# adaLN slots of the feed-forwards: eight running sums with an outside sum by TensorE, or row-wise multiply-and-sum on VectorE

## The chip, the core and the metric

The kernel runs on one core of a Trainium2 chip. The metric is the device time of one execution in microseconds (us). Engines are named as in the profile: PE is TensorE (PEld its weight loads), DVE is VectorE, ACT is ScalarE, POOL is GpSimd, SP is SyncE, which here issues nearly all the loads.

## The reference

Two transformer blocks of two layers each run over 256 tokens of 1024 features. Each layer has an adaLN vector of 6 x 1024 outputs, made from one condition vector; the change is only about how these vectors come about.

```python
def adaln(c, w_mod, b_mod):
    mod = jax.nn.silu(c) @ w_mod + b_mod          # [1, 6*1024]
    return jnp.split(mod, 6, axis=-1)             # shift, scale, gain; twice

def modulate(x, g, shift, scale):
    return rmsnorm(x, g) * (1.0 + scale[:, None, :]) + shift[:, None, :]

def swiglu(h, wg, wu, wd):
    return (jax.nn.silu(h @ wg) * (h @ wu)) @ wd
...
    # layer_ab, layer_c (block one): mixer, then
    h = modulate(x, norm_ffn, sh_f, sc_f)
    return x + g_f[:, None, :] * swiglu(h, wg, wu, wd)
```

Block one is `layer_ab` (a linear recurrence and sparse attention) and `layer_c` (attention over selected keys), each followed by `swiglu` with 2816 hidden features. Block two has two layers with a context of 256 more tokens, low-rank attention and 16 experts; its adaLN is computed for two condition vectors (tokens and context).

## The kernel before

Activations lie feature-major: 128 features on the partitions, 8 chunks, 256 tokens along the free axis. A dense product in fp32 is made from two rounded halves: `split` copies 1024 columns of a weight to a high half on ACT (`wsh`, L308) and subtracts it on DVE for the low half (`wsl`, L309), with three buffers of each; `mm3` (L316 to L318) then multiplies high by high, high by low and low by high.

A feed-forward (`ffn`) takes its norm first: the sum of squares on PE, a transpose to a narrow layout on DVE (L559), a reciprocal square root in tiny DVE operations of 8 columns (L567, L536 to L546), the way back (L577, L579), and then `h` (L604 on DVE, L605 on ACT, L606 on DVE). The gate/up part has 11 steps; each loads one 2 MB slot and makes two pairs of chunks, gate and up, of 24 products each, with the activation behind them (L973 on ACT, L974 and L975 on DVE, L976 on ACT, L977 on DVE). The down part has 8 chunks of 66 products. FFN0 runs from about 170 us of the trace, FFN1 from about 505 us; layer 1 of block one is between them, block two starts at about 710 us.

Loads go through `slot`: a ring of four places of 2 MB in block one, filled in the order of the program by SP's queue. A load waits until the place's former content has been read, and every load behind it on SP's queue waits with it. Where work on the former content has been put off, `slot` has that work emitted before it takes the place.

The adaLN vectors of the four layers (`mod0`, `mod1`, `ada0`, `ada1`) are 12 slots of 512 outputs each, made by the generator `mods` one after another, wherever the code calls `fill`. A slot on TensorE is 8 products of 128x32 by 128x512 (L458, 16 records in the trace), added up on DVE or ACT (L464, L462), and a transpose of all such slots at the end (L471). A slot on DVE is put off into a queue, `vq`, of eight pieces for each condition vector: one multiply-and-add of 128x512 each (L425; the first piece is ACT's, L428), and at the end four products with a column of ones on TensorE (L434) and an addition (L435). `split` takes three pieces from the queue after each split in gate/up (`VU`), one in down (`VD`). Strings set where slots go: `PF` after each gate/up step, `FD` before each down chunk, `NF` at the norms, `L1F` in layer 1's attention; a digit is that many slots on TensorE, `a` one on DVE.

Of the kernel before, what the change touches and what calls it, by code (L numbers as in the profile page):

```python
# [19 lines left out]
MC = 2  # L20
# [22 lines left out]
VU = 3  # L43
VD = 1
FD = 'a0aa0000,00000000'.split(",")
# [6 lines left out]
PF = [e for e in '02a0a00a0a0,2000000000a'.split(",")]  # L52
# [3 lines left out]
L1F = '0010020100000000'  # L56
NF = '021'
# [91 lines left out]
def layout(i):  # L149
# [30 lines left out]

    w = i["l0_w_in"]
# [53 lines left out]
class Kern:  # L235
# [41 lines left out]
    def slot(self, src, cuts=1):  # L277
        n = src.shape[-1]
        self.nslot += 1
        # a place is taken anew only when the work put off has had what is in it  # L280
        while any(e[2] is not None and self.nslot - e[2] >= len(self.rq_) for e in self.vq):
            self.pump(1)
        pool, tag, bufs = self.rq_.pop(0)
# [14 lines left out]
    def drop_ring(self, h):  # L298
        cm, mine = h
        self.pump(len(self.vq))  # L300
        self.rq_ = [e for e in self.rq_ if e not in mine]
        self.drop(cm)

    def split(self, src, n, tag=None):
# [5 lines left out]
        self.pump(self.vn)  # L310
# [25 lines left out]
    def setup(self):  # L336
# [20 lines left out]
        self.pend, self.vq, self.vn, self.nslot = None, [], 0, 0  # L357
        self.known = {}
# [47 lines left out]
    def mods(self, name, zname, bias):  # L406
        """The adaLN columns of one layer, a slot of 512 at a time; yields take the engine for the next."""
# [6 lines left out]
        for s in range(12):  # L414
            vec = yield
            w = self.slot(self.I[name][s].rearrange("p k n -> p (k n)"), MC if name == "mod0" and s == 3 else 1).rearrange("p (k n) -> p k n", n=512)
            z = self.zc[zname]
            old = self.mark("mods")
            if vec:
                zp, ts = self.zp, []  # L420

                def part(k, i, w=w, z=z, ts=ts, zp=zp):
                    c = 31 + 16 * i
                    if k:
                        nc.vector.scalar_tensor_tensor(ts[i], w[:, k, :], z[:, k, c:c + 1], ts[i], op0=ALU.mult, op1=ALU.add)  # L425
                    else:
                        ts.append(self.t(zp, [128, 512], F32, f"modv{i}", 1))
                        nc.scalar.activation(ts[i], w[:, 0, :], AF.Copy, scale=z[:, 0, c:c + 1])  # L428

                def fin(ts=ts, s=s):  # L430
                    for i, t in enumerate(ts):
                        tp = self.ps("t")
                        for q in range(4):
                            nc.tensor.matmul(tp[:, q:q + 1], t[:, q * 128:(q + 1) * 128], self.ones[:, 0:1], start=True, stop=True)  # L434
                        nc.vector.tensor_tensor(m[:, i, 4 * s:4 * s + 4], tp[:, :4], self.cols[:, o + 4 * s:o + 4 * s + 4], op=ALU.add)  # L435
                    self.known[name].add(s)

                for k in range(8):
                    for i in range(n):
                        self.vq.append((lambda k=k, i=i, part=part: part(k, i), "mods", self.nslot))  # L440
                f, old_ = self.vq[-1][0], fin
                self.vq[-1] = (lambda f=f, fin=fin: (f(), fin()), "mods", self.nslot)
                self.mark(old)
# [4 lines left out]
            if self.zp is None:  # L448
                # late: a window of its own
# [39 lines left out]
    def pump(self, n):  # L489
        """Some of the work put off for the vector engine."""  # L490
        for _ in range(min(n, len(self.vq))):
# [3 lines left out]
            self.mark(old)  # L495

# [8 lines left out]
    def flush(self, name=None, part=None):  # L505
        """The last steps of the adaLN columns, put off until they are asked for."""
        if name is None:
            self.pump(len(self.vq))
# [5 lines left out]
        while not need <= self.known[name]:  # L514
            assert self.vq, (name, part)
            self.pump(1)

# [16 lines left out]
    def rsqrt(self, y, c, t):  # L534
# [3 lines left out]
        # y (1 - e) ** -0.5 with e = 1 - c y y below 0.07, a polynomial to the last bits; scaled to a leading one  # L538
# [9 lines left out]
    def sums(self, x, gain=None):  # L548
        """Sum of the squares over the features; tokens 32 b + p on partition p, column b."""
# [23 lines left out]
    def spread(self, y):  # L573
        """A column layout of tokens back to a row on every partition."""
# [46 lines left out]
    def dense_iter(self, src, n, h, use, lead=0, cuts=1):  # L621
        """use(j, psum) for every 128-column chunk j of a packed weight [128, n, 1024]; the first ones by turns."""
# [18 lines left out]
    def lead(self, w, h):  # L641
        """Some chunks by turns, as the parts of h come."""
# [8 lines left out]
    def warm(self, n):  # L651
        """Products that keep the tensor engine's clock up while it waits."""
# [9 lines left out]
    def gelu(self, dst, src, n, eng=None):  # L662
        """dst = 2 * gelu(src)"""
# [35 lines left out]
    def lru1(self, axp, lruw):  # L699
# [5 lines left out]
        for c in range(4):  # L705
# [7 lines left out]
            # tr -> t = tanh(log_a / 2), rec -> 1 / (1 - t) = (1 + a) / 2  # L713
# [15 lines left out]
            # a = 1 + 2 t / (1 - t)  # L729
# [3 lines left out]
            # y = h * gelu(gate), gate holds 2 * gelu  # L733
# [10 lines left out]
    def attend(self, qch, qb, kz, mask, vtok, voff, gate, yps, first, last):  # L744
        """One pair of heads (one of either group), one block of queries."""
# [30 lines left out]
    def layer0(self, fill, r0, xr):  # L776
# [74 lines left out]
        # compressed keys and values  # L851
# [24 lines left out]
        # attention over the compressed keys  # L876
# [23 lines left out]
        for r in range(4):  # L900
# [28 lines left out]
            if r == LQ:  # L929
                self.mark("l0 lru")  # L930
                # xc -> sqrt(-t)
# [14 lines left out]
    def ffn(self, l, mname, fill):  # L946
        nc, I = self.nc, self.I
        self.mark("ffn")
        r = self.rstd(self.xT, 1024)
# [8 lines left out]
        self.vn = VU  # L958
# [24 lines left out]
        self.vn = VD  # L983
# [12 lines left out]
        self.vn = 0  # L996
        self.drop(fpc)

    def layer1(self, fill):
# [44 lines left out]
        def select(qb):  # L1044
# [14 lines left out]
            # causal keys only: v * m + (m - 1) * 3e38  # L1059
# [46 lines left out]
    def run_a(self):  # L1106
# [12 lines left out]
        def fill(n, vec=False):  # L1119
            if isinstance(n, str):  # L1120
                n, vec = (int(n), False) if n.isdigit() else (ord(n) - 96, True)
# [11 lines left out]
        if EN:  # L1133
            # the context's place is free
# [17 lines left out]
    def rs_cols(self, ss, n, inv):  # L1152
        """columns (ss * inv + eps) ** -0.5"""
# [10 lines left out]
    def rope(self, dst, src, t):  # L1164
        """src [128 tok, m, 64] -> dst"""
# [19 lines left out]
    def raw(self, nm, i=0):  # L1185
        """The slot of a packed weight, loaded at its first use."""
# [12 lines left out]
    def tm(self, acc, w, n, off, tiles, ks):  # L1199
        """Token-major products: acc[t][:, c0:] += h[t]^T w for some chunks of features."""  # L1200
# [19 lines left out]
    def st_v(self, sis):  # L1220
        """v and f"""
# [20 lines left out]
    def st_t(self, sis):  # L1242
        """Low-rank parts of queries, keys and values."""
# [53 lines left out]
    def st_k(self, si):  # L1297
        """Keys and values."""
# [39 lines left out]
    def st_q(self, si):  # L1338
        """Queries."""
# [36 lines left out]
        # (192 (ms + eps)) ** -0.5: norm and score scale  # L1376
# [12 lines left out]
    def st_s(self, si):  # L1389
        """Spatial gating."""  # L1390
# [15 lines left out]
    def st_f(self, si):  # L1406
        """Fourier transforms; the second half of the frequencies mirrors the first."""
# [20 lines left out]
    def st_a(self, si, hd):  # L1428
        """Attention of one head."""
# [30 lines left out]
    def st_w(self, sis, half=None):  # L1460
        """Output product, onto the residual."""
# [17 lines left out]
    def logits(self, i, s0):  # L1479
        """Four feature blocks' share of the logits of the scaled tokens, and of the sum of squares (row 16 of a quarter)."""  # L1480
# [16 lines left out]
    def st_x(self, si):  # L1497
        """Normed and modulated tokens (0) or context (1)."""
# [30 lines left out]
    def run_plan(self, plan):  # L1529
        """The stages of a layer of block 2 in the order in which they are traced."""  # L1530
# [73 lines left out]
    def st_p(self, si):  # L1604
        """What the route needs besides the tokens: scaled router weights, the shift's share of the logits."""
# [20 lines left out]
    def route(self, sis):  # L1626
        """Experts' choice and the tokens of the first experts, for some sets at once; in stages."""
# [301 lines left out]
```

## Time and profile before

| | |
|---|---|
| median of 3 runs | 1565.83 us (1565.28 to 1566.07) |
| profiled execution, span | 1562.8 us |
| outside the span, against the median | 3.0 us |
| PE busy | 1452.5 us (93%) |
| DVE busy | 845.4 us (54%) |
| ACT busy | 580.9 us (37%) |
| L458, the adaLN slots on TensorE | 624 records, 91.7 us busy |

"Busy" is the time in which an engine has at least one instruction in flight. The chain of work that ended last is followed backwards from the last instruction, so that its shares say on which engine the end of the program hung. Matmul records overlap; a record of 0.28 us follows the one before it after 0.12 us where PE runs without a break.

### The profile page before, as it was taken

How to read it: one execution, taken by the hardware profiler on the slowest of the kernel's cores; microseconds unless marked ns; L12 is line 12 of the kernel's file. 1: busy time of each engine (PE TensorE's matmuls, PEld its weight loads, DVE VectorE, ACT ScalarE, POOL GpSimd, SP SyncE). 2: the span in 40 equal slices, each digit the busy share in tenths (PEclk: the TensorE clock that was granted, in tenths of full speed). 3: DMA queues.
4: the chain of work that ended last, by engine and by line, in shares of the span. 5: the costliest groups of instructions: out<-in, count | busy, mean ns of one | idle time of the engine just before them, and what ended most of it. 6: DMA issues, size and time to landing. Idle time of an engine off the chain costs nothing.

```text
span 1562.8 us, 25643 instructions
## 1 busy us (share of the span) xinstructions
PE 1452.5 (93%) x10566; PEld 1001.6 (64%) x10566; DVE 845.4 (54%) x1960; ACT 580.9 (37%) x1184; POOL 5.6 (0%) x15
## 2 busy tenths in 40 slices
PE   5999999999999999999999998999998989897665
PEld 2975899998957899996754784434433655642211
DVE  5668787766776668745766542323224765421011
ACT  3455444443455444543654441111102564310000
POOL 0000000000000000000000000000000000000000
PEclk9999999999999999999999998999999999999888
DMA  9647767577464844545386976899994544799998
GB/s 398 259 181 288 269 225 294 195 291 289 144 262 164 312 174 155 189 170 189 115 317 226 402 308 250 332 414 386 412 368 168 201 175 182 313 429 427 427 427 346
DMA packets 33380, 432.55 MB, mean 277 GB/s; under 512 B 3696, under 2 KB 4336, under 8 KB 5872
## 3 DMA queue, kind: packets, MB, share of 16 engines
q1 hardware_dynamic: 32400, 429.92, 69.3%
q8 instruction: 83, 1.36, 0.3%
q10 hardware_dynamic: 864, 1.00, 0.2%
q14 instruction: 33, 0.27, 0.0%
HBM read 429.86 MB, written 1.05 MB: 276 GB/s over the span
## 4 chain that ended last, share of the span: by engine, by line
PE 79%; DMA 9%; DVE 6%; ACT 2%; issue 1%; POOLq 0%; DVEq 0%; ACTq 0%; SPq 0%
PE g L316 14%; PE g L317 14%; PE g L318 14%; PE g L1770 7%; PE y L1807 5%; DMA raw<-in_md_dram 4%; PE t L458 4%; DMA h<-in_mgu_dram 3%; DMA raw<-in_mgu_dram 3%; PE m L1770 2%; PE t L1729 2%; PE y L1441 1%; PE y L1439 1%; PE g L1457 1%; PE y L751 1%; PE y L1729 1%
## 5 line engine op out<-in xcount | busy, mean ns | idle before, releaser
L308 ACT ACTIVATE wsh<-raw 128x1024 fp32r<-128x1024 f32 (+4 forms) x236 | 243.2, 1033 | 323.9 <-PE g L317 228.3
L309 DVE TENSOR_TENSOR wsl<-raw,wsh 128x1024 fp32r<-128x1024 f32 (+4 forms) x236 | 280.2, 1189 | 147.5 <-ACT wsh L308 146.8
L316 PE MATMUL g<-h,wsh 128*128 128x256 f32 x1072 | 304.6, 286 | 2.8 <-ACT h L597 2.4
L318 PE MATMUL g<-h,wsl 128*128 128x256 f32 x1072 | 304.7, 285 | 0.6 <-DVE wsl L309 0.6
L317 PE MATMUL g<-h,wsh 128*128 128x256 f32 x1072 | 304.3, 285 | 0.1
L316 PEld LDWEIGHTS g<-h,wsh 128*128 128x128 f32 x1072 | 205.3, 192 | 8.0 <-ACT h L597 2.6
L318 PEld LDWEIGHTS g<-h,wsl 128*128 128x128 f32 x1072 | 206.0, 192 | 1.9 <-DVE wsl L309 1.0
L317 PEld LDWEIGHTS g<-h,wsh 128*128 128x128 f32 x1072 | 206.0, 193 | 1.9 <-DVE h L606 1.2
L1770 PE MATMUL g<-raw,xs 128*32 128x512 f32 x1232 | 166.9, 632 | 20.8 <-DMA raw<-in_mgu_dram 20.2
L1807 PE MATMUL y<-raw,a 128*32 128x512 f32 x736 | 100.4, 634 | 9.8 <-DMA raw<-in_md_dram 8.3
L1770 PEld LDWEIGHTS g<-raw,xs 128*32 128x32 f32 x1232 | 39.1, 113 | 106.2 <-issue 71.0
L316 PE MATMUL g<-gh,wsh 128*128 128x256 f32 x352 | 100.3, 285 | 0.0
L318 PE MATMUL g<-gh,wsl 128*128 128x256 f32 x352 | 99.7, 283 | 0.0
L317 PE MATMUL g<-gl,wsh 128*128 128x256 f32 x352 | 99.7, 283 | 0.0
L458 PE MATMUL t<-raw,zc 128*32 128x512 f32 x624 | 91.7, 621 | 5.5 <-DMA raw<-in_mod_dram 5.4
L1734 ACT ACTIVATE xs<-t,modada,ra 128x128 f32<-128x128 f32 x32 | 14.6, 457 | 152.5 <-PE t L1729 109.1
L316 PEld LDWEIGHTS g<-gh,wsh 128*128 128x128 f32 x352 | 67.5, 192 | 0.8 <-DVE modada L483 0.4
L317 PEld LDWEIGHTS g<-gl,wsh 128*128 128x128 f32 x352 | 67.5, 192 | 0.4 <-issue 0.4
L318 PEld LDWEIGHTS g<-gh,wsl 128*128 128x128 f32 x352 | 67.5, 192 | 0.4 <-issue 0.4
L1807 PEld LDWEIGHTS y<-raw,a 128*32 128x32 f32 x736 | 23.4, 112 | 63.7 <-issue 42.5
L1779 ACT ACTIVATE a<-g 128x512 f32<-128x512 f32 x12 | 7.2, 597 | 148.2 <-PE g L1770 148.2
L1732 DVE TENSOR_SCALAR xs<-t,ra,modada 128x128 f32<-128x128 f32 x32 | 13.1, 410 | 88.7 <-PE t L1729 50.4
(482 smaller groups left out, 2364.2 us busy)
## 6 DMA issues: line engine op xcount, KB each, us to landing
raw<-in_mgu_dram SPq DMA_DIRECT2D x61, 2048.0 KB, 13.1
raw<-in_md_dram SPq DMA_DIRECT2D x28, 2048.0 KB, 10.8
raw<-in_mod_dram SPq DMA_DIRECT2D x23, 2048.0 KB, 8.7
raw<-in_ada_dram SPq DMA_DIRECT2D x23, 2048.0 KB, 8.5
raw<-in_ffgu_dram SPq DMA_DIRECT2D x22, 2048.0 KB, 8.6
raw<-in_ffd_dram SPq DMA_DIRECT2D x16, 1408.0 KB, 5.9
raw<-in_win_dram SPq DMA_DIRECT2D x6, 2048.0 KB, 11.1
raw<-in_wo_dram SPq DMA_DIRECT2D x6, 2048.0 KB, 10.4
```

What stands on the lines that cost most here:

```text
L308: self.nc.scalar.activation(hi, src, AF.Copy)
L309: self.nc.vector.tensor_tensor(lo, src, hi.bitcast(F32), op=ALU.subtract)
L316: mm(out, ah, bh, start=first, stop=False)
L317: mm(out, ah, bl, start=False, stop=False)
L318: mm(out, al, bh, start=False, stop=last)
L458: nc.tensor.matmul(acc[32 * j:32 * j + 32, :], zw[:, k, :], w[:, k, :], start=(k < 4), stop=(k >= 4))
L751: nc.tensor.matmul(sc, qch[:, qb * 128:(qb + 1) * 128], kz[:, :, :nk], start=False, stop=True)
L1439: nc.tensor.matmul(sc, self.qT[:, hd, ts], self.kT[:, hd, :nk], start=True, stop=False)
L1441: nc.tensor.matmul(sc, self.qrT[s2, hd // 2, ts], self.krT[s2, hd // 2, :nk], start=False, stop=True)
L1729: nc.tensor.matmul(ps, s["ht"][:, t, k * 128:(k + 1) * 128], oh[:, t, :], start=(t == 0), stop=(t == 1))
L1770: nc.tensor.matmul(banks[si][u][32 * e:32 * e + 32, :], xs[:, k, e * 32:e * 32 + 32], raw[:, u * 2048 + e * 512:u * 2048 + e * 512 + 512], ...
L1807: nc.tensor.matmul(ys[si][32 * e:32 * e + 32, :], hts[si][:, f * 128 + 32 * e:f * 128 + 32 * e + 32], raw[:, (fj * 4 + e) * 512:(fj * 4 + ...
```

## The change

Slots given to DVE are now made row by row. The weights of all four layers are packed a second time, transposed (`mod0t` and so on), so that outputs lie on the partitions and the 1024 inputs along the free axis. One `tensor_tensor_reduce` (L438 of the new kernel, "ISA" in the rows below, followed by a row of 128x1 that writes the accumulated value) multiplies 128x1024 weights by the condition vector, which stands on every partition, and adds up each row: four of these make a slot for one condition vector, eight for two. Products with ones on TensorE are no longer needed. The product itself is written over the weights, or to a scratch tile in bfloat16 (`a512`) where the weights are needed again. The condition vector on all partitions (`crow`) is loaded at first use in a feed-forward by a DMA on ACT's queue and passed through ACT (Tanh) and DVE (L541).

The strings are new: eight DVE slots in FFN0's gate/up (four on DVE and two on TensorE before), three in its down part, six in FFN1's gate/up, where two on TensorE and one on DVE had been. `L1F` has one slot instead of four. In all 17 slots are on DVE instead of eight, and nine fewer on TensorE (two of these in layer 1 of block two). A split now takes 0.8 pieces from the queue. Code for slots on GpSimd is there and not used.

```diff
-VU = 3
-VD = 1
-FD = 'a0aa0000,00000000'.split(",")
+VU, VD = (0.8, 0.8), (0.8, 0.8)
+PU, PD = (0, 0), (0, 0)
+FD = ['d d d 0 0 0 0 0'.split(), '0 0 0 0 0 0 0 0'.split()]
...
-PF = [e for e in '02a0a00a0a0,2000000000a'.split(",")]
+PF = ['0 0 d d d d d d d d 0'.split(), 'd d d d d d 0 0 0 0 0'.split()]
...
-L1F = '0010020100000000'
-NF = '021'
+L1F = '0000000100000000'
+NF = '0,2,1'.split(',')
...
+        o[nm + "t"] = np.ascontiguousarray(w.T.reshape(12, 4, 128, 1024).transpose(0, 2, 1, 3))
...
-        self.pump(self.vn)
+        self.paced()
...
-                def part(k, i, w=w, z=z, ts=ts, zp=zp):
...
-                        nc.vector.scalar_tensor_tensor(ts[i], w[:, k, :], z[:, k, c:c + 1], ts[i], op0=ALU.mult, op1=ALU.add)
...
+                zr, ni = self.row(zname), 1 if name == "ada1" and s >= 4 else n
+                todo = [(q, i) for q in range(4) for i in range(ni)]
...
+                        junk = w[:, q, :] if last else self.w([128, 1024], "a512", NA5, BF16)
+                        nc.vector.tensor_tensor_reduce(junk, w[:, q, :], zr[:, i, :], 0.5, self.cols[:, o + 4 * s + q:o + 4 * s + q + 1],
+                                                       ALU.mult, ALU.add, m[:, i, 4 * s + q:4 * s + q + 1])
...
+    def paced(self):
+        self.vc += self.vn
...
+        self.pump(int(self.vc))
...
+    def row(self, zname):
...
+            nc.scalar.dma_start(z, self.I["crow"][:, :n] if n == 1 else self.I["crow"][:, 1:])
+            for i in range(n):
+                t = self.t(self.zr, [128, 1024], F32, "modp", 1)
+                nc.scalar.activation(t, z[:, i, :], AF.Tanh, scale=0.5)
+                nc.vector.scalar_tensor_tensor(z[:, i, :], t, 1.0, z[:, i, :], op0=ALU.add, op1=ALU.mult)
```

The final order on an engine is set by a scheduler, and it shows at three places. The first is DVE at FFN1's norm, from the transpose to the first row of `h`. Before:

```order
L559 STREAM_TRANSPOSE a_901_5590<-t_5565 128x256
L567 TENSOR_SCALAR rsc_5594<-t_5592 128x8
L536 TENSOR_SCALAR rsy_5596<-rsc_5594 128x8
L537 TENSOR_SCALAR rsy_5596<-rsy_5596 128x8
L539 TENSOR_TENSOR rst_5597<-rsy_5596 128x8
L540 TENSOR_TENSOR rst_5597<-rst_5597,rsc_5594 128x8
```

Now, in the same stretch (`raw_917` is the first slot of `ada0` on DVE, `crow` the condition vectors):

```order
L613 STREAM_TRANSPOSE a_879_5473<-t_5448 128x256
L438 ISA raw_917_5685,modada_787_5015<-raw_917_5685,crowc_918_5687,cols_63 128x1024
L438 ISA modada_787_5015 128x1
L621 TENSOR_SCALAR rsc_5477<-t_5475 128x8
L497 TENSOR_REDUCE modmod_415_2455<-t_5494 128x4x3
L590 TENSOR_SCALAR rsy_5479<-rsc_5477 128x8
L438 ISA a_945_5868,modada_787_5015<-raw_917_5685,crowc_918_5687,cols_63 128x1024
L438 ISA modada_787_5015 128x1
L591 TENSOR_SCALAR rsy_5479<-rsy_5479 128x8
L498 TENSOR_TENSOR modmod_415_2455<-modmod_415_2455,cols_63 128x12
L438 ISA raw_917_5685,modada_787_5015<-raw_917_5685,crowc_918_5687,cols_63 128x1024
```

Two more such rows follow before L595, so that five stand between the transpose and the reciprocal square root; one more stands between two rows of `h`, and two behind the last row of `h`.

The second place is SP at the end of FFN1's gate/up (`ffgu` is a gate/up slot, `ffd` a down slot). Before:

```order
L288 DMA raw_1046_6728<-in_ffgu_dram 128x4096
L288 DMA raw_1061_6858<-in_ffgu_dram 128x4096
L288 DMA raw_1076_6988<-in_ffgu_dram 128x4096
L288 DMA raw_1091_7118<-in_ada_dram 128x4096
L288 DMA raw_1111_7178<-in_ffd_dram 128x2816
```

Now (`raw_1016` is the last DVE slot of FFN1, `raw_1070` the gate/up slot of step 9, which takes the same place of the ring):

```order
L294 DMA raw_1016_6401<-in_ada0t_dram 128x4096
L294 DMA raw_1053_6681<-in_ffgu_dram 128x4096
L294 DMA raw_1085_6947<-in_ffgu_dram 128x4096
L294 DMA raw_1118_7126<-in_ffd_dram 128x2816
L294 DMA raw_1130_7229<-in_ffd_dram 128x2816
L294 DMA raw_1070_6817<-in_ffgu_dram 128x4096
```

The load of step 9 stands behind that of step 10 and two of the down part.

The third place is DVE at the eighteenth pair of FFN1's gate/up and the start of the nineteenth, which is the first of step 9. Now:

```order
L1029 SCALAR_TENSOR_TENSOR a_1069_6810<-a_1069_6810,g_6754 128x256
L438 ISA raw_1016_6401,modada_787_5015<-raw_1016_6401,crowc_918_5687,cols_63 128x1024
L438 ISA modada_787_5015 128x1
L584 SCALAR_TENSOR_TENSOR acol_7957<-modada_787_5015,cols_63 128x8
L1030 SCALAR_TENSOR_TENSOR a_1069_6810<-a_1069_6810,g_6785 128x256
L1032 TENSOR_TENSOR gl_5554<-a_1069_6810,gh_5553 128x256
L315 TENSOR_TENSOR wsl_6820<-raw_1070_6817,wsh_6819 128x1024
L315 TENSOR_TENSOR wsl_6849<-raw_1070_6817,wsh_6848 128x1024
```

The last piece of `raw_1016` stands in the middle of the eighteenth pair, and the first split of `raw_1070` is the next thing but two that DVE does. Before, at the same place (`raw_1061` is the slot of step 9, `raw_1091` the DVE slot of that time):

```order
L309 TENSOR_TENSOR wsl_6861<-raw_1061_6858,wsh_6860 128x1024
L977 TENSOR_TENSOR gl_5663<-a_1053_6788,gh_5662 128x256
L425 SCALAR_TENSOR_TENSOR modv_1115_7185<-raw_1091_7118,zc_11_94,modv_1115_7185 128x512
L425 SCALAR_TENSOR_TENSOR modv_1118_7215<-raw_1091_7118,zc_11_94,modv_1118_7215 128x512
L309 TENSOR_TENSOR wsl_6890<-raw_1061_6858,wsh_6889 128x1024
L974 SCALAR_TENSOR_TENSOR a_1060_6852<-a_1060_6852,g_6798 128x256
```

There the first two splits of step 9 stood ahead of the eighteenth pair's first activation row.

## Rows read from the trace of the kernel before

**Rows 1.** Page part 1: engine, busy us (share), instructions.
```profile
PE 1452.5 (93%) x10566; PEld 1001.6 (64%) x10566; DVE 845.4 (54%) x1960; ACT 580.9 (37%) x1184; POOL 5.6 (0%) x15
```
**Rows 2.** Page part 4: shares of the chain by line.
```profile
PE g L316 14%; PE g L317 14%; PE g L318 14%; PE g L1770 7%; PE y L1807 5%; DMA raw<-in_md_dram 4%; PE t L458 4%; DMA h<-in_mgu_dram 3%; DMA raw<-in_mgu_dram 3%; PE m L1770 2%; PE t L1729 2%; PE y L1441 1%; PE y L1439 1%; PE g L1457 1%; PE y L751 1%; PE y L1729 1%
```
**Rows 3.** Chain in layer 1's attention: start us, us, what.
```profile
445.45 1.83 PE t L458 x10
...
456.07 3.56 PE t L458 x30
```
**Rows 4.** Chain in layer 1 of block two.
```profile
1285.83 1.85 PE t L458 x16
```
**Rows 5.** Chain at the outside sums, FFN0 gate/up and FFN1 end.
```profile
221.81 0.79 PE t L434 x8
...
667.65 1.68 PE t L434 x16
```
**Rows 6.** PE in time, start of FFN0: start us, us, instruction, [idle before, releaser].
```profile
175.74 3.62 PE L458 MATMUL t<-raw,zc 128*32 128x512 f32 x26
179.76 0.62 PE L316 MATMUL g<-h,wsh 128*128 128x256 f32 x3 [0.40 <-ACT h L605]
180.31 1.06 PE L458 MATMUL t<-raw,zc 128*32 128x512 f32 x6
```
**Rows 7.** PE in time, start of FFN1.
```profile
505.63 4.48 PE L458 MATMUL t<-raw,zc 128*32 128x512 f32 x34
```
**Rows 8.** Chain in FFN1's first steps.
```profile
519.41 0.99 PE t L458 x8
...
523.47 0.99 PE t L458 x6
```
**Rows 9.** DVE in time, a pair and a half of FFN1 without slot work.
```profile
531.47 1.23 DVE L309 TENSOR_TENSOR wsl<-raw,wsh 128x1024 fp32r<-128x1024 f32 x1 [0.60 <-ACT wsh L308]
532.61 0.42 DVE L977 TENSOR_TENSOR gl<-a,gh 128x256 fp32r<-128x256 f32 x1
...
537.24 1.23 DVE L309 TENSOR_TENSOR wsl<-raw,wsh 128x1024 fp32r<-128x1024 f32 x1 [0.61 <-ACT wsh L308]
```
**Rows 10.** The same in a stretch with slot work.
```profile
613.76 1.41 DVE L425 SCALAR_TENSOR_TENSOR modv<-raw,zc,modv 128x512 f32<-128x512 f32 x2
```
**Rows 11.** Windows: stretch, us, busy PE, PEld, DVE, ACT, POOL, clock, DMA.
```profile
529.00:541.00 12.00, 12.00 (x102) 12.00 (x102) 7.57 (x11) 5.40 (x8) 0.00 (x0) 1.00 0.68 260
...
613.00:625.00 12.00, 12.00 (x102) 12.00 (x102) 11.98 (x19) 5.40 (x8) 0.00 (x0) 1.00 0.37 136
```
**Rows 12.** DVE in time, FFN1's norm.
```profile
504.81 0.45 DVE L559 STREAM_TRANSPOSE a<-t 128x256 f32<-128x256 f32 x1
...
506.75 0.17 DVE L541 TENSOR_SCALAR rst<-rst 128x8 f32<-128x8 f32 x1
...
509.05 1.27 DVE L604 SCALAR_TENSOR_TENSOR a<-xT,acol,rsr 128x256 f32<-128x256 f32 x3
```
**Rows 13.** DVE in time, the norm in layer 1 of block two.
```profile
1206.42 0.44 DVE L559 STREAM_TRANSPOSE a<-y 128x256 f32<-128x256 f32 x1
1206.78 1.18 DVE L309 TENSOR_TENSOR wsl<-raw,wsh 128x1024 fp32r<-128x1024 f32 x1
...
1211.71 1.28 DVE L604 SCALAR_TENSOR_TENSOR a<-xT,acol,rsr 128x256 f32<-128x256 f32 x3
```
**Rows 14.** PE in time behind that norm.
```profile
1212.79 0.79 PE L316 MATMUL g<-wsh,hh 128*128 128x512 f32 x1 [5.49 <-ACT hh L605]
```
**Rows 15.** The window around it, columns as in rows 11.
```profile
1210.00:1220.00 10.00, 7.21 (x20) 4.49 (x20) 7.98 (x23) 5.92 (x16) 0.00 (x0) 0.66 0.00 0
```
**Rows 16.** DMA issues, 226 to 238 us: out<-in, queue, count, KB, us to landing.
```profile
raw<-in_ffgu_dram SPq DMA_DIRECT2D x1, 2048.0 KB, 8.2
raw<-in_mod_dram SPq DMA_DIRECT2D x1, 2048.0 KB, 13.0
```
**Rows 17.** ACT in time, the split's copy.
```profile
530.38 1.06 ACT L308 ACTIVATE wsh<-raw 128x1024 fp32r<-128x1024 f32 x1 [1.54 <-issue]
```

More of the change, by code (lines that the diff above doesn't have):

```diff
@@ L179, in layout @@
     o["ada1"] = kchunks(i["w_ada_2"][1], 512)
+    for nm, w in (("mod0", i["l0_mod_w"]), ("mod1", i["l1_mod_w"]), ("ada0", i["w_ada_2"][0]), ("ada1", i["w_ada_2"][1])):
+        o[nm + "t"] = np.ascontiguousarray(w.T.reshape(12, 4, 128, 1024).transpose(0, 2, 1, 3))
+    o["crow"] = np.ascontiguousarray(np.broadcast_to(np.stack([i["c"][0], i["c_2"][0], i["c_ctx_2"].reshape(-1)])[None], (128, 3, 1024)))
     w = i["l0_w_in"]
@@ L282, in slot @@
             self.pump(1)
+        while any(self.nslot - e[2] >= len(self.rq_) for e in self.pq):
+            self.pump_p(1)
         pool, tag, bufs = self.rq_.pop(0)
@@ L415, in mods @@
             vec = yield
-            w = self.slot(self.I[name][s].rearrange("p k n -> p (k n)"), MC if name == "mod0" and s == 3 else 1).rearrange("p (k n) -> p k n", n=512)
+            w = self.slot(self.I[name + ("t" if vec else "")][s].rearrange("p k n -> p (k n)"), MC if name == "mod0" and s == 3 else 1)
+            w = w.rearrange("p (k n) -> p k n", n=1024 if vec else 512)
             z = self.zc[zname]
@@ L430, in fin @@
[L430 to L440, printed above, removed]
@@ L495, in pump, with pump_p, drain @@
             self.mark(old)
+    def pump_p(self, n):
+        for _ in range(n):
+            if self.pf and (len(self.pf) == 2 or not self.pq):
+                act, pr = self.pf.pop(0)
+                act(pr)
+            while self.pq and len(self.pf) < 2:
+                pool, act, _ = self.pq.pop(0)
+                self.pf.append((act, pool()))
+    def paced(self):
+        self.vc += self.vn
+        self.pc += self.pn
+        self.pump(int(self.vc))
+        self.pump_p(int(self.pc))
+        self.vc %= 1
+        self.pc %= 1
+    def row(self, zname):
+        nc = self.nc
+        if zname not in self.rowz:
+            self.drain()
+            n = 2 if zname == "c2" else 1
+            z = self.t(self.zr, [128, n, 1024], F32, "crow" + zname, 1)
+            nc.scalar.dma_start(z, self.I["crow"][:, :n] if n == 1 else self.I["crow"][:, 1:])
[3 more added lines that the diff above has]
+                nc.vector.scalar_tensor_tensor(z[:, i, :], t, 1.0, z[:, i, :], op0=ALU.add, op1=ALU.mult)
+            self.rowz[zname] = z
+        return self.rowz[zname]
+    def drain(self):
+        self.pump(len(self.vq))
+        while self.pq or self.pf:
+            self.pump_p(1)
     def flush_pe(self):
@@ L507, in flush @@
         if name is None:
-            self.pump(len(self.vq))
+            self.drain()
             self.flush_pe()
@@ L514, in flush @@
         while not need <= self.known[name]:
-            assert self.vq, (name, part)
+            assert self.vq or self.pq or self.pf, (name, part)
             self.pump(1)
+            self.pump_p(1)
     def mcol(self, name, part, k, i=0):
@@ L948, in ffn @@
         self.mark("ffn")
+        self.zr, zrc = self.pool(f"zr{l}", 1)
         r = self.rstd(self.xT, 1024)
@@ L995, in ffn @@
             nc.vector.scalar_tensor_tensor(self.xT[:, j, :], o, self.mcol(mname, 5, j), self.xT[:, j, :], op0=ALU.mult, op1=ALU.add)
-        self.vn = 0
-        self.drop(fpc)
+        self.vn = self.pn = 0
+        self.drain()
+        self.drop(fpc, zrc)
     def layer1(self, fill):
@@ L1120, in fill @@
             if isinstance(n, str):
-                n, vec = (int(n), False) if n.isdigit() else (ord(n) - 96, True)
+                for c in n:
+                    fill(int(c) if c.isdigit() else 1, False if c.isdigit() else c)
+                return
             for _ in range(n):
```

35 lines of the change are left out of this document (24 added, 11 removed).

## The prediction

> **What bounds the kernel now.** I read the page's busy times first: PE works 1452.5 us of 1562.8, DVE 845.4 [rows 1]. The chain that ended last says the same: it hangs on PE, with 42% in the three products of the split (L316 to L318) and 4% in the adaLN slots, L458 [rows 2]. So PE is the bound, and what leaves PE is worth its time where PE had nothing to wait for. The next view is therefore the chain at the places where slots are removed. In layer 1's attention three of four slots go; they lie on the chain, sixteen records (a slot) in some 1.85 us [rows 3, 4]. At the norms of the feed-forwards PE in time says something else: in FFN0 26 of 32 records fill the 4.0 us in which PE waits for `h` [rows 6], in FFN1 34 records do [rows 7], and only 6 records (1.06 us) and 8 and 6 (0.99 us each) stand between products [rows 6, 8]. The removed outside sums (L434) are on the chain, 0.79 us for one condition vector, 1.68 us for two [rows 5].
>
> Then I asked what DVE can take. A feed-forward's pair of chunks takes PE 5.77 us (537.24 less 531.47), and DVE has two splits in it that follow at 1.14 us and three rows of 0.42 us [rows 9]: 3.54 us. In twelve microseconds without slot work DVE is busy 7.57 us, with it 11.98 us, and PE 12.00 us in both [rows 11]. So DVE may be full without PE losing anything, as long as its splits stay ahead of PE.
>
> **The price of the new operation.** No row has a multiply-and-sum with a result per row (the row of 128x1 behind it is an instruction too). The nearest is the split: 1024 columns, two fp32 operands from SBUF, 1.14 us from start to start [rows 9]; with a tiny row of 0.17 us [rows 12] behind it, 1.3 us. The other neighbour is the old piece, two of 512 columns in 1.41 us [rows 10]; with 0.17 us, 1.6 us. I take 1.3 us, bounds 1.14 to 1.6.
>
> Two such old pieces also read two fp32 operands, and at 1.41 us for 1024 columns they run at nearly the split's rate [rows 9, 10]. [...]
>
> **FFN0.** The exposed six records go: -1.06 us. The gap of 4.0 us is now bare. After a bare gap of 5.49 us in block two [rows 14] the granted clock is 0.66 over ten microseconds [rows 15]. [...] For the shorter gap here I take 1.0 us (0 to 2.0). On ACT's queue the condition row's load and its Tanh now stand ahead of `h`. The load (512 KB) starts at about 174 us and takes between a quarter and all of a 2 MB slot's 8.2 us [rows 16], the Tanh some 1.06 us as the copy of the same width [rows 17]: ready between 177 and 183 us, where `h` was due at 179.2. I take +1.0 us (0 to 4). Seven outside sums go: 7 x 0.8 = -5.6 us. In gate/up 31 new operations cost DVE 40 us beside 22 x 3.54 = 78 us, 118 us against PE's 127 us; the order keeps splits two to three ahead, so nothing. Before the second down chunk ends five of them stand in a row and the split after it has lost its lead: one split and one row late (1.14 + 0.42), +1.6 us (0 to 3). Together -3.1 us.
>
> **Layer 1 of block one.** Three slots at 1.85 us: -5.5 us. In the new order two splits of the output product have moved into the chain of the key selection on DVE: 2 x 1.14 = +2.3 us where nothing hides it (0 to 2.3). Together -3.2 us.
>
> **FFN1, the norm.** From the transpose to `h` DVE took 504.81 to 509.05, 4.24 us, in 0.17 us steps [rows 12]. In the new order five of the new operations stand inside, and three tiny rows, while one addition (0.6 us) is gone: 5 x 1.3 = 6.5, less 0.5 us that hides behind PE's turn: +6.0 us. That such inserted rows do lengthen the norm is to be seen in block two: with two splits inside, the same way took 1206.42 to 1211.71, 5.29 us [rows 13]. One more stands between rows of `h`: +1.3 us (to 3 if its weights land late). PE has one slot left to fill a gap of some 10 us, so more than 5.49 us is bare, and the clock costs +2.0 us as above. The two exposed half slots go, -2.0 us, and the outside sum, -1.7 us. Together +5.6 us (2 to 9).
>
> **FFN1, gate/up.** Two things meet here. DVE has 35 new operations in the sixteen pairs left: 45.5 + 56.6 = 102 us against PE's 92 us. And weights of a DVE slot keep their place of the ring until the last of eight pieces has run, at 0.8 pieces to a split two and a half steps later. Every load behind the waiting one on SP's queue waits too. The order shows where this bites.
>
> At the ninth pair's start the last piece of a slot runs; only then go out the next DVE slot's load and, behind it, that of gate/up step 5. Two loads one behind the other landed after 8.2 and 13.0 us [rows 16]. The second's landing and 1.06 us of copy [rows 17] are over 14.1 us after the issue, which is about 2.6 us into the ninth pair; PE is done with the tenth at 11.5 us. That is 5.2 us at most, 0.3 us if it lands as a single load; I take +4.0 us.
>
> Worse is step 9, pair nineteen. Its slot takes the place of the last DVE slot, whose last piece stands in the middle of pair eighteen, behind the gate chunk's activation: half a pair (2.9), the Tanh and L1029 (0.8), the piece (1.3), so 5.0 us into the pair. The load then needs 8.2 us and the copy 1.06 us: PE goes on 14.3 us after the start of a pair that it ended at 5.8: +8.5 us of idle PE, with no slot left to fill it. The clock after it as in block two: +2.0 us. Bounds 6 and 13 us for both. FFN1 in all: 5.6 + 4.0 + 10.5 = +20.1 us.
>
> **Block two, layer 1.** Two slots fewer; one was on the chain [rows 4], the other beside waits. -2.4 us, bounds -3.9 and 0. From 1320 us on loads set the pace, and the same bytes are loaded.
>
> **Sum.** -3.1 - 3.2 + 20.1 - 2.4 = +11.4 us on the span of 1562.8 us: 1574.2 us. The runs' median is 3.0 us above the span, so the time is 1577.2 us. With single terms at their bounds it goes from 1568 to 1590.
>
> **Rivals.** *The late loads don't bite.* If DVE gets through its pieces earlier than I count, or a lone 2 MB load lands in much less than 8 us, pairs ten and nineteen start in time: 1577.2 - 4.0 - 10.5 = 1562.7 us. For it: DVE has spare time in FFN0 and waits had not stopped PE there. Against it: the last piece of the place stands where it stands, and 8.2 us is longer than one pair.
>
> *The nine slots and the sums pay, and the norm is cheap too.* Then also the norm's five pieces run while DVE would wait for something else, and its clock stays: 1562.7 - 8 = about 1555 us, faster than before. Against it stands the order of rows 12's stretch, where the pieces are between steps that need each other.
>
> *The new operation costs double,* 2.28 + 0.17 = 2.45 us. Then FFN0's gate/up is 31 x 2.45 + 78 = 154 us against 127 us on PE, +27; its down part +6; the norm of FFN1 6 x 1.15 = +7; its gate/up 35 x 2.45 + 57 = 142 us against 92 us, +50 instead of the +4 of pair ten. Together 27 + 6 + 7 + 46 = 86 us more, 1577.2 + 86 = 1663 us. It decides from 1.5 us a piece on in FFN0, since 127 - 78 = 49 us is what DVE has for 31 pieces. [...] Against it: the old pieces, which come next in form, are far from it [rows 10].
>
> **How the numbers follow.** The forecast gets 0.58, the late loads that don't bite 0.12, the gain 0.17, the double price 0.13. The predicted time is the forecast's. The range leaves out the double price and the lower end of the gain: 1552 to 1590 us. A measurement of this kernel tells some 0.2% (3.1 us) from no change. Of the forecast 0.53 is slower by more than that and 0.05 is not; 1562.7 us is divided between faster (0.06), the same (0.05) and slower (0.01); the gain is all faster and the double price all slower. That makes faster 0.24, the same 0.09, slower 0.67.
>
> **What would show it.** The new rows at 1.2 to 1.4 us on DVE; at FFN1's norm some 10 us from transpose to `h`, and a granted clock under 1 behind it; in FFN1 two waits of PE for the copy (`wsh`), the longer one of some 8 us behind the load of step 9, right after the activation of pair eighteen; none of that size in FFN0; no L434. Wrong would be the argument if PE ran through FFN1's gate/up without a wait, or if new rows were at 2.4 us.

## The result, and the profile after

The changed kernel takes 1576.76 us (median of 4 runs, 1576.54 to 1580.62) against 1565.73 us for the kernel before: a ratio of 1.0082, 95% interval 1.0068 to 1.0096. It is 11 us slower; 1577.2 us had been forecast. The profiled execution has a span of 1574.9 us, 12.1 us more than before. Two executions in a slow state (3540 us for the kernel before, 6557 us for the spread version below) are left out of all ratios and comparisons.

The first view is the page's busy times, which answers [rows 1].

```profile
PE 1438.1 (91%) x10343; PEld 1000.4 (64%) x10346; DVE 905.4 (57%) x2065; ACT 579.3 (37%) x1177; POOL 5.6 (0%) x15
```

PE works 14.4 us less, as nine slots (31 are left of 40) and the outside sums are gone, and yet the program ends later: PE now waits more. By DVE's transposes at five of the norms (L559 before, L613 after) the program falls into six stages; a stage runs from one of these transposes to the next.

| stage, by its first transpose | before | after | difference | forecast |
|---|---|---|---|---|
| up to FFN0's norm | 174.9 | 175.3 | +0.4 | 0 |
| FFN0 | 205.3 | 200.9 | -4.4 | -3.1 |
| layer 1 of block one | 124.6 | 121.5 | -3.1 | -3.2 |
| FFN1 | 208.9 | 229.7 | +20.8 | +20.1 |
| layer 0 of block two | 492.7 | 491.7 | -1.0 | 0 |
| layer 1 of block two, to the span's end | 356.3 | 355.8 | -0.5 | -2.4 |

So 7 us had been gained when FFN1 began, and FFN1 alone lost 21. Where it lost them is told by PE's waits, the next view (engine, line, waited for: us in total, times, longest); lines 322 to 324 are the three products, L314 the copy of the split, L315 its subtraction:

```profile
...
PE g L322 <- ACT wsh L314: 9.9, 3, 8.1
PE g L322 <- ACT h L659: 9.2, 3, 4.9
...
PE g L324 <- DVE wsl L315: 3.1, 3, 1.2
```

Before, PE had not waited more than 0.8 us for any copy or subtraction in the program. The wait of 8.1 us is at step 9 of FFN1's gate/up. The chain shows what it hung on (start us, us, what):

```profile
617.85 0.13 PE g L324
618.01 0.39 ACT a L1028
618.42 0.42 DVE a L1029
618.90 1.06 issue
620.08 7.68 DMA raw<-in_ffgu_dram
627.91 0.89 issue
628.80 1.05 ACT wsh L314
```

DVE in time shows the piece in which the load was waiting (a row of 128x1 is the accumulator's, as its own instruction):

```profile
618.42 0.42 DVE L1029 SCALAR_TENSOR_TENSOR a<-a,g 128x256 f32<-128x256 f32 x1
618.76 1.28 DVE L438 CUSTOM_DVE_ANT_0 raw<-raw,crowc,cols 128x1024 f32<-128x1024 f32 x1
619.97 0.08 DVE L438 DVE_READ_ACCUMULATOR2_ANT modada<- 128x1 f32 x1
...
628.92 3.50 DVE L315 TENSOR_TENSOR wsl<-raw,wsh 128x1024 fp32r<-128x1024 f32 x3 [6.71 <-ACT wsh L314]
```

The piece ends at 619.97; the load of the next gate/up slot into the same place goes out at 620.08, lands at 627.8, and only then comes the copy. PE had ended pair eighteen at 620.8. Ahead of the piece the chain runs over PE and ACT: DVE was not late here, it had to wait for pair eighteen's gate chunk, behind whose activation the piece stands in the order. The norm is the other place. On DVE, answering [rows 12]:

```profile
497.70 0.45 DVE L613 STREAM_TRANSPOSE a<-t 128x256 f32<-128x256 f32 x1
498.08 1.24 DVE L438 CUSTOM_DVE_ANT_0 raw<-raw,crowc,cols 128x1024 f32<-128x1024 f32 x1
499.24 0.08 DVE L438 DVE_READ_ACCUMULATOR2_ANT modada<- 128x1 f32 x1
499.24 0.16 DVE L621 TENSOR_SCALAR rsc<-t 128x8 f32<-128x8 f32 x1
...
504.77 0.17 DVE L595 TENSOR_SCALAR rst<-rst 128x8 f32<-128x8 f32 x1
...
506.58 1.28 DVE L658 SCALAR_TENSOR_TENSOR a<-xT,acol,rsr 128x256 f32<-128x256 f32 x3
```

From transpose to the first row of `h` it is 8.88 us instead of 4.24. The price of the new operation stands in its group of rows (duration ns min/median/max):

```profile
L438 DVE CUSTOM_DVE_ANT_0 raw<-raw,crowc,cols x68: 1244/1279/1286, 186.5 to 618.8; 128x1024 f32<-128x1024 f32 x68
L438 DVE DVE_READ_ACCUMULATOR2_ANT modada<- x48: 79/82/88, 490.5 to 620.0; 128x1 f32 x48
```

In the norm one starts at 500.88 and the next instructions, the accumulator's row and a tiny step, at 502.08: 1.20 us. The windows (columns as in rows 11) show the granted clock behind the three bare gaps, FFN0's norm, FFN1's norm and step 9:

```profile
180.00:186.00 6.00, 5.88 (x30) 5.73 (x31) 6.00 (x14) 3.09 (x8) 0.04 (x1) 0.59 0.00 0
...
508.00:518.00 10.00, 10.00 (x68) 10.00 (x68) 9.69 (x21) 4.91 (x10) 0.00 (x0) 0.77 0.63 269
620.00:630.00 10.00, 1.75 (x11) 1.25 (x9) 2.05 (x6) 2.58 (x4) 0.00 (x0) 0.76 0.69 289
630.00:640.00 10.00, 10.00 (x64) 10.00 (x65) 5.27 (x7) 3.48 (x5) 0.00 (x0) 0.73 0.17 41
```

### The profile page after: what moved, and what is told of

It reads as the page before. It is cut to its first block, busy times and chain, and to the rows that moved or that the text cites. A ratio compares the mean times of both kernels' runs of the same rounds, so it can differ in the third digit from the quotient of the medians.

```text
span 1574.9 us, 25243 instructions
## 1 busy us (share of the span) xinstructions
PE 1438.1 (91%) x10343; PEld 1000.4 (64%) x10346; DVE 905.4 (57%) x2065; ACT 579.3 (37%) x1177; POOL 5.6 (0%) x15
## 4 chain that ended last, share of the span: by engine, by line
PE 74%; DMA 12%; DVE 10%; ACT 3%; issue 1%; SPq 0%; ACTq 0%; POOLq 0%; DVEq 0%
PE g L322 13%; PE g L324 12%; PE g L323 12%; PE g L1828 7%; DMA raw<-in_md_dram 5%; PE y L1865 5%; DMA raw<-in_mgu_dram 5%; PE t L473 3%; DVE wsl L315 2%; PE m L1828 2%; PE t L1787 2%; PE y L1499 1%; PE y L1497 1%; PE g L1515 1%; DMA raw<-in_mod_dram 1%
## 5 line engine op out<-in xcount | busy, mean ns | idle before, releaser
L314 ACT ACTIVATE wsh<-raw 128x1024 fp32r<-128x1024 f32 (+4 forms) x232 | 238.4, 1032 | 323.1 <-PE g L323 228.2
L315 DVE TENSOR_TENSOR wsl<-raw,wsh 128x1024 fp32r<-128x1024 f32 (+4 forms) x232 | 274.5, 1188 | 109.0 <-ACT wsh L314 108.3
L322 PE MATMUL g<-h,wsh 128*128 128x256 f32 x1072 | 309.3, 290 | 22.0 <-ACT wsh L314 9.9
L324 PE MATMUL g<-h,wsl 128*128 128x256 f32 x1072 | 308.4, 289 | 3.2 <-DVE wsl L315 3.1
L323 PE MATMUL g<-h,wsh 128*128 128x256 f32 x1072 | 308.4, 289 | 0.0
L322 PEld LDWEIGHTS g<-h,wsh 128*128 128x128 f32 x1072 | 210.2, 197 | 26.3 <-ACT wsh L314 12.0
L324 PEld LDWEIGHTS g<-h,wsl 128*128 128x128 f32 x1072 | 209.7, 196 | 5.1 <-DVE wsl L315 4.0
L323 PEld LDWEIGHTS g<-h,wsh 128*128 128x128 f32 x1072 | 210.3, 196 | 1.0 <-issue 0.7
L1828 PE MATMUL g<-raw,xs 128*32 128x512 f32 x1216 | 166.3, 635 | 20.8 <-DMA raw<-in_mgu_dram 20.1
L438 DVE CUSTOM_DVE_ANT_0 raw<-raw,crowc,cols 128x1024 f32<-128x1024 f32 x68 | 86.2, 1279 | 0.2 <-DMA raw<-in_mod1t_dram 0.2
L473 PE MATMUL t<-raw,zc 128*32 128x512 f32 x496 | 74.4, 644 | 6.1 <-DMA raw<-in_mod_dram 5.8
## 6 DMA issues: line engine op xcount, KB each, us to landing
raw<-in_md_dram SPq DMA_DIRECT2D x29, 2048.0 KB, 11.3
```

The lines of the kernel that those rows point to most:

```text
L314: self.nc.scalar.activation(hi, src, AF.Copy)
L315: self.nc.vector.tensor_tensor(lo, src, hi.bitcast(F32), op=ALU.subtract)
L322: mm(out, ah, bh, start=first, stop=False)
L323: mm(out, ah, bl, start=False, stop=False)
L324: mm(out, al, bh, start=False, stop=last)
L438: nc.vector.tensor_tensor_reduce(junk, w[:, q, :], zr[:, i, :], 0.5, self.cols[:, o + 4 * s + q:o + 4 * s + q + 1], ALU.mult, ALU.add, m[: ...
```

## The experiments

The theory: FFN1's loss is made of places of the ring that the pieces hold too long (step 9 above all), and of pieces that stand in the norm. The rival: DVE simply has too much work in FFN1, so that any forty or fifty new pieces would cost about that. For it speaks that from PE's first gate/up product to the last piece (507.7 to 620.1 us) DVE is busy 109.8 of 112.4 us. Executions of one kernel differed by up to 9 us here, so that single times are good to a few microseconds only; the stages of the traces are compared, which is where the theories differ.

### The norm's pieces cut short

```diff
+WIDTH = lambda name, s: 8 if (name, s) == ('ada0', 1) else 1024
...
+                        ww = WIDTH(name, s)
...
-                        nc.vector.tensor_tensor_reduce(junk, w[:, q, :], zr[:, i, :], 0.5, ...
+                        nc.vector.tensor_tensor_reduce(junk[:, :ww], w[:, q, :ww], zr[:, i, :ww], 0.5, ...
```

> The pieces of one DVE slot only (slot 1 of ada0, the one that stands in FFN1's norm) are cut to 8 of 1024 columns, so that slot's outputs are left incomplete; all else is the changed kernel. Theory (the norm is lengthened by pieces between its steps): from transpose to the first row of h 4.3 us instead of 8.9, the clock lost behind it halved, some 1576.8 - 7 = 1570 us (1568 to 1572), and PE's wait of 8 us at gate/up step 9 stays, since that place of the ring is still held by the last DVE slot. Rival (DVE's load as a whole sets FFN1): eight pieces of 1.2 us less are taken from the waits at pair ten and nineteen, which shrink or go, and the time falls by up to 10 us, to 1567.

Measured: 1573.09 us. The way from the transpose to `h` is 3.77 us (two lines were added to this kernel, so L615 is the transpose and L660 the first row of `h`):

```profile
497.09 0.45 DVE L615 STREAM_TRANSPOSE a<-t 128x256 f32<-128x256 f32 x1
...
500.86 1.27 DVE L660 SCALAR_TENSOR_TENSOR a<-xT,acol,rsr 128x256 f32<-128x256 f32 x3
```

The clock is 1.00 from 498 to 518 us, where the changed kernel had 0.72 and 0.77. PE's wait at step 9 is still there, 6.7 us. FFN1 takes 225.1 us, 4.7 less than the changed kernel and not the 7 expected: what the norm gives back is partly taken by the next waits, since splits that start earlier meet the same loads (one wait for a copy at the tenth pair is now 3.2 us, where it had been 1.4). So the norm's pieces cost what their rows show, and the waits behind remain. The chain ahead of step 9's load now looks different:

```profile
606.96 0.42 DVE a L1032
607.38 1.20 DVE a L440
...
613.06 1.20 DVE a L440
...
614.61 1.20 DVE raw L440
...
615.84 7.83 DMA raw<-in_ffgu_dram
```

From 573 to 616 us it runs mostly over DVE (L440 are the pieces here), which is busy 42.0 of these 43.1 us. So with the norm 5 us shorter it is DVE's amount of work that sets when the place comes free: in this version the rival holds for that stretch.

### The last DVE slot made on TensorE

```diff
-PF = [..., 'd d d d d d 0 0 0 0 0'.split()]
+PF = [..., 'd d d d d 0 0 0 0 0 1'.split()]
```

> The last of FFN1's six DVE slots is made on TensorE at the end of gate/up instead. In the order step 9's load no longer stands behind a DVE slot's pieces; instead step 6's slot takes the place of the third DVE slot (raw_976), whose last piece ends with pair eleven, and its first split is due at the start of pair thirteen. Theory (a wait is load plus copy less the pairs in between): no wait at step 9 (-8 and -2 of clock), a new one of 8.2 + 1.06 less one pair of 5.8 and about 1 us, 3 to 5 us, at pair thirteen, one slot more on PE +1.9: 1576.8 - 10 + 5 + 2 = 1574 us (1570 to 1576). Rival (DVE's load): no wait longer than one split's time anywhere, 1567 us.

Measured: 1579.06 us, and FFN1 no shorter than in the changed kernel. The wait at step 9 is gone, and one of 8.8 us stands at pair thirteen, where 3 to 5 us had been expected. Its place was forecast from the order, its size not. The chain there:

```profile
581.83 11.35 DMA raw<-in_ffgu_dram
593.17 0.02 issue
593.21 0.04 issue
593.26 0.07 ACT wsh L314
593.33 0.89 issue
594.22 1.05 ACT wsh L314
```

The last piece in the place (`raw_976`) ended at 581.80; the load went out at 581.83, behind another of 580.3, and took 11.35 us instead of the 8.2 that I had set for a lone one. PE had work until 585.5: 581.8 + 11.35 + 1.06 - 585.5 = 8.7 us, the wait. The rule (load plus copy, less what PE still has) gives the size when the right load time and the right remaining work are put in; I had put in a whole pair of work and a lone load. The rival's forecast falls: eight pieces fewer on DVE, and PE waits longer.

### The pieces taken faster

```diff
-VU, VD = (0.8, 0.8), (0.8, 0.8)
+VU, VD = (0.8, 1.25), (0.8, 0.8)
```

> The changed kernel with one number changed: in FFN1's gate/up a split takes 1.25 pieces from the queue instead of 0.8. The 48 pieces, their places in the ring and the order up to pair fourteen stay; the last piece of the last DVE slot now stands at the end of pair seventeen instead of in the middle of eighteen. Theory (step 9 waits for a place that the last piece holds): its load goes out some 3.5 us earlier against PE, the wait falls from 8.1 to 4 to 5.5 us, and the time to about 1573.5 us (1572 to 1575). Rival (DVE's load in FFN1, which is the same): the same waits or longer ones, 1576 to 1579 us.

Measured: 1575.83 us. With the same 48 pieces, the same places and the same amount of work on DVE the load of step 9 goes out at 618.34 instead of 620.08. Counted from FFN1's norm that is 1.4 us earlier, while PE ends pair eighteen 2.2 us later, and the wait is 4.5 us:

```profile
618.34 7.69 DMA raw<-in_ffgu_dram
...
627.08 1.05 ACT wsh L314
```

FFN1 takes 227.0 us, 2.7 less than in the changed kernel: 1.4 by the earlier load, and the rest behind the wait. That is the theory's sign and place, but less than its size: the wait shrank more than the time did, because PE came later; its waits for a subtraction between 580 and 620 us grew from 1.9 to 2.8 us. The time as a whole fell by one microsecond instead of three, to a time between the two forecasts, which one execution can't tell from none; the stage and the load's issue carry this one.

### All pieces cut short

```diff
+WIDTH = lambda name, s: 8
...
```

> All 92 pieces are cut to 8 of 1024 columns (the outputs of the DVE slots are left incomplete): the change without the time of its new operation. Theory (the nine slots and the outside sums were on PE's path, and what the pieces cost in FFN1 is more than that): no wait of PE for a split or a copy over 1 us in FFN1, and 1565.7 - 4.4 (FFN0) - 3 to -5 (layer 1) - 2 (FFN1, with a bare norm) - 1.6 (block two) = 1553 us (1549 to 1556). Rival (the removed slots lay beside waits and were worth little): 1561 to 1566 us.

Measured: 1552.94 us. FFN0 takes 199.1 us, layer 1 120.7, FFN1 205.7, and PE waits for no split in FFN1. So what the change takes off PE is worth some 12 us against the kernel before, and the pieces took 24 us back. This run shortens the pieces and frees the places earlier at once, so it doesn't tell the two apart.

### FFN1 as it was

```diff
-PF = [..., 'd d d d d d 0 0 0 0 0'.split()]
+PF = [..., '2 0 0 0 0 0 0 0 0 0 d'.split()]
```

> FFN1 gets the slots that it had in the kernel before (two on TensorE after step 0, one on DVE, now after step 10 and in the new form), so three slots more are left to block two; FFN0 and layer 1 stay changed. Theory (what the change gains ahead of FFN1 is kept, and the loss is FFN1's): FFN1's norm is at 497.7 us as in the changed kernel, FFN1 takes 207 to 210 us, block two up to 3 x 1.9 us more: 1576.8 - 20.85 + 1 to 6 = 1557 to 1562 us. Rival (the loss was prepared by FFN0's slots or the new place of the loads): over 1566 us.

Measured: 1569.45 us, where 1557 to 1562 had been expected. FFN1 takes 207.3 us, as the theory had it: FFN0's slots had prepared nothing. But the three slots that are left over fall to block two, and its last layer takes 369.6 us instead of 355.8: 13.8 us for three slots, not up to 5.7. All three run there on the chain, which has 11.3 us of slot products instead of 3.8 (five slots in that layer instead of two): 7.5 us. Most of the rest is again a load. The chain ahead of that layer's attention, and PE's longest wait in front of the expert part:

```profile
1244.43 7.24 DMA raw<-in_wo_dram
1251.76 1.06 ACT wsh L314
```

```profile
PE t L1351 <- ACT a L1345: 6.0, 1, 6.0
```

The load of the output weights (`wo`) went out only at 1244.4, 46 us after that layer's norm instead of 30 in the changed kernel, behind the loads of two more slots on SP's queue and when its place had been read, and took its 7.2 us bare. ACT's copy waited for it, and behind the copy the rows for which PE then stood idle for 6.0 us, where the changed kernel has no wait over 1 us for these rows. The two together are about as large as the 13.8 us; other differences, the clock of 0.89 from 1230 to 1260 us among them, were not added up. A slot left to block two thus costs more than its products.

### FFN0's norm filled

```diff
-PF = ['0 0 d d d d d d d d 0'.split(), ...
+PF = ['0 0 d d d d d d d 0 0'.split(), ...
-NF = '0,2,1'.split(',')
+NF = '1,2,1'.split(',')
```

> One of FFN0's DVE slots goes to TensorE, into the norm's bare gap of 4 us. Theory (a bare gap of 4.0 us costs clock): the granted clock from 180 to 186 us is 1.00 instead of 0.59, and FFN0 takes 2 us less, 199 us instead of 200.9; the slot itself is hidden in the gap. FFN1's loss stays: 1574.5 us (1573 to 1576). Rival (the low clock there is not from the gap, or comes with the condition row's DMA): clock and time of FFN0 unchanged.

Measured: 1577.06 us, so nothing is gained in the end. The clock is as the theory says:

```profile
180.00:186.00 6.00, 5.58 (x46) 5.38 (x46) 6.00 (x14) 2.69 (x7) 0.04 (x1) 1.00 0.72 303
```

With 1.92 us of slot products and the 0.66 us of transposes behind them in the gap, PE's clock is 1.00 where it had been 0.59. FFN0 takes 199.5 us, 1.4 less, and layer 1 another 0.9 less. FFN1 is 0.5 longer (a wait of 9.2 us at step 9), and the last layer 3.0 us longer; PE's waits for expert weights grew there by 1.7 us, and where the rest lies was not followed. The four executions of the spread version below differ by 9 us among themselves, so a difference of this size between single executions tells nothing. So the gap's price is shown, the fate of the gain is not.

### FFN1's slots spread

```diff
-PF = [..., 'd d d d d d 0 0 0 0 0'.split()]
+PF = [..., '0 0 d 0 0 d 0 0 d 0 0'.split()]
-FD = [..., '0 0 0 0 0 0 0 0'.split()]
+FD = [..., 'd 0 0 d 0 0 0 0'.split()]
-NF = '0,2,1'.split(',')
+NF = '0,2,2'.split(',')
```

> FFN1's slots spread: one more on TensorE in the bare norm, DVE slots only after gate/up steps 2, 5 and 8 and before down chunks 0 and 3, all work done. In the order no piece stands in the norm, splits stay at least two ahead in gate/up but for pair twelve and thirteen, and each load of gate/up is issued two pairs or more ahead of its first split. Theory (places held and pieces in the norm, not DVE's load, cost FFN1 its 21 us): FFN1 takes no more than before's 209 us, 1576.8 - 21 - 0 to 3 = 1555 us (1552 to 1559), under both kernels. Rival (any forty new pieces in FFN1 cost about what they take beside a full PE): 1565 to 1572 us.

Measured: four executions from 1551.62 to 1560.49 us, a ratio of 0.9958 to the kernel before, 95% interval 0.9941 to 0.9974. The profiled one, the fastest of the four, has FFN1 at 204.6 us, 25 less than in the changed kernel, and PE waits nowhere in it for a split, a copy or `h`. Forty full pieces stand in it, and it is even a microsecond shorter than FFN1 with all pieces cut short (205.7), whose norm has one slot less on TensorE. The stage repeats well: the version below has the same FFN1, its profiled execution is the slowest of its four, and FFN1 takes 204.8 us there. DVE is as busy as it can be in places, and PE doesn't notice:

```profile
613.00:625.00 12.00, 12.00 (x102) 12.00 (x102) 12.00 (x21) 5.57 (x8) 0.00 (x0) 1.00 0.30 107
```

So forty pieces in FFN1 can cost nothing, and the rival as it was put falls: where the pieces stand and how long they hold a place decides. The number within gate/up is not excluded as a part of the cause, since the order moved it too: 30 pieces start there instead of 40, the other ten in the down part, and DVE is busy 114.8 of its 127.8 us, where the changed kernel had 126.3 us of work on DVE in 147.7. No version here has forty full pieces in gate/up and no wait.

### Both norms filled

```diff
-NF = '0,2,2'.split(',')
+NF = '1,2,2'.split(',')
```

> The spread version with one slot more on TensorE, in FFN0's norm; all work done, so twelve slots' room in FFN0 and five on DVE in FFN1. Theory: the spread version less FFN0's clock loss of 2 us and whatever the one slot fewer in block two gives (up to 1.9): 1553 us (1550 to 1557). Rival (filling costs what it gives): the same as the spread version, 1556 us.

Measured: 1547.01 us (1543.8 to 1548.63), a ratio of 0.9875, 95% interval 0.9858 to 0.9891: 18 us faster than the kernel before and better than expected. FFN0 takes 199.8 us, FFN1 204.8 us, the last layer 354.5 us. It is the fastest version of this study. Why it gained ten microseconds on the spread version's median where three to four had been expected is not shown: the two profiled executions are only 3 us apart, most of it in the last layer.

## Why the prediction was right

**FFN1** was the term that decided (+20.1 set, +20.8 measured), and its waits came where they had been set, but that the sum is so close is partly luck. *Step 9* was set at 8.5 us of idle PE and 2.0 of clock. The wait is 8.1 us; the load took 7.68 us (8.2 set) and went out when the piece ended, 0.8 us ahead of PE's end of the pair, as the working has it. The clock cost somewhat more: over the ten microseconds from the first product on, 628.9 to 638.9 us, it is 0.67, and products follow at 0.213 us instead of 0.12 up to 635.4 us, a loss of some 2.8 us. The place cost 10.9 us, then, for the 10.5 set. No run shows the 2.0 us of clock that were set here and at the norm, nor the 1.0 us in FFN0: they were my estimates. In the trace before, products of 128x512 behind the gap of 5.49 us [rows 14] follow at 0.43 us up to 1216.8 us and at 0.23 us after that (1217.1, 1218.5), which makes some 1.8 us lost; in the trace after, 2.8 us are lost here, 2.1 at the norm and 2.1 in FFN0. *The norm* was set at +6.0 us, and one piece more between rows of `h` at +1.3. DVE's way became 4.6 us longer, since between pieces the tiny steps follow at 0.08 us instead of 0.2 [rows 12] and so took less than counted. For the piece between rows of `h` no wait of PE shows. The clock behind it (0.77 over ten) lost about 2.1 us, products following at 0.213 us from 507.7 to 512.5 us; 2.0 had been set. PE's first product came 4.6 us later behind the transpose; with that loss, and less the 3.7 us of slot products and outside sum that left PE, the term is some +3.0 us and not +5.6. *Pair ten* was set at 4.0 us. PE idled 2.5 us there between 560 and 580 us; the load for which it waited went out at 560.0 and landed 7.9 us later, not 13.0: the DVE slot's load ahead of it, which I had counted as going out at the same moment, had gone out at 551.2 already. The second load of [rows 16] was the wrong neighbour:

```profile
551.22 0.33 SPq L294 DMA_DIRECT2D raw<-in_ada0t_dram  x1
...
560.03 7.89 DMA raw<-in_ffgu_dram
...
566.00:576.00 10.00, 7.46 (x48) 6.75 (x47) 10.00 (x15) 3.65 (x5) 0.00 (x0) 0.83 0.57 241
```

The first line is from SP in time, the second from the chain, the third a window. With the clock (0.83 from 566 to 576; products follow at 0.213 us from 571.3 to 574.0 us, some 1.2 us lost), which had not been set here, the place cost 3.7 us, about as much as was set. That is luck: the load was as quick as a single one, for which the working gave a wait of 0.3 us; but it went out only 7.7 us ahead of PE's end of pair ten, not 8.9, and two shorter waits (0.8 and 0.4 us) followed the first of 1.4. Two waits for a subtraction of 0.8 and 1.1 us at about 597 and 601 us, where DVE itself was late, had not been set at all; they and step 9 made up for most of what the norm cost less. The terms as measured come to 19.5 of the 20.8 us; where the rest lies was not followed.

**The new operation** was set at 1.3 us, from the split's row. It took 1.28 us, 1.20 from start to start, with 0.08 us for the accumulator beside the next step. The rival on the doubled price falls: two fp32 operands and an accumulated result, and the rows are nearly as short as a split's 1.23 [rows 9]. Its 2.45 us a piece were my estimate, two splits and a tiny step, and no run shows them. A row of L541, with a scalar and two tensors and no accumulated result, took 1.22 us for 128x1024.

**FFN0** was -3.1 and is -4.4 us, and the sum is closer than its parts. The condition row landed early: its load took 3.8 us, and Tanh began at 177.4 us, two microseconds before `h` was due, so the +1.0 us for it was nothing. The bare gap cost 2.1 us and not 1.0: products follow at 0.213 us instead of 0.12 for 4.8 us from 180.1 on. Filling the gap brought the clock back to 1.00, and FFN0 down by 1.4 us. The stall that had been set in the down part (+1.6) doesn't show as a wait of PE. **Layer 1** was -3.2 and is -3.1 us; PE's first wait for the mask (`imask`) is 1.6 us, for the 2.3 that the two moved splits had been given; another of 1.2 us for a subtraction, at 480 us, had not been set. **Block two** was the term that was off: -2.4 us set, -0.5 measured in the last layer, and -1.0 in the layer before, where nothing had been forecast. I had priced a slot there by its 1.85 us on the chain; the run with FFN1 as it was shows that loads count there beside products, which that row doesn't tell.

The rivals: *the late loads don't bite* was refuted by the chain at 620 us, *the nine slots and the sums pay* is true of what leaves PE (12 us with all pieces cut short) and was overlaid by FFN1. It took the spread order to make it come true.

## What to carry to other kernels

Work put off onto an idle engine costs more than that engine's time where it holds a buffer that a prefetch needs (at step 9, 8.1 us of idle PE behind a piece of 1.28 us): look for the last reader of each place, and count the wait as load plus consumer's first step, less the work that the bound engine still has. If the idle engine becomes full by it, as DVE was here, its lateness comes on top (waits of 0.8 and 1.1 us for a subtraction). Put such work behind norms and other chains of short dependent steps, not between them (with five pieces FFN1's norm took 8.88 us from transpose to `h` instead of 4.24), and give the bound engine something of its own in their gaps, since a bare gap of 4.0 us cost another 2.1 us, at a granted clock of 0.59. Before judging a move by its sum of busy times, compare nearly the same work in another order: here 17 slots on DVE lost 11 us, and 16, in other places and with one slot more on TensorE in each of the two norms, gained 18.

## What was not expected of the hardware

In the same part of the program a 2 MB load took 7.68 us where the load ahead of it (1.4 MB) had gone out 3.25 us earlier, and 11.35 us behind another of 2 MB that had gone out 1.5 us earlier. Behind a bare gap of 4.0 us on PE the granted clock was 0.59 over the next six microseconds, and 2.1 us were lost, about the 2.0 us that had been estimated for a gap of 5.49 us [rows 14, 15]; with 1.92 us of slot products in it, and 0.66 us of transposes behind them, the clock was 1.00.
